# The last projection of a hybrid conformer and attention block: two full halves against seven products of quarters

## The chip, the core and the metric

The kernel runs on one core of a Trainium2 chip. The metric is the time of one execution on the device, in microseconds (us). Before the change it was 2436.01 us, the median of three runs (2435.82 to 2436.03).

## The reference, cut to what matters

The layer takes x of 2048 tokens by 1024 channels, runs a convolution branch and an attention branch, merges them into y (2048 x 1024), multiplies y by the output matrix, scales each output channel by a gate that is computed from the conditioning vector c, and adds x. Only the last lines are touched here:

```python
    mod = jax.nn.silu(c) @ w_ada + b_ada
    shift, scale, gate = jnp.split(mod, 3, axis=-1)
    ...
    y = jax.nn.sigmoid(m_conv) * y_conv + jax.nn.sigmoid(m_attn) * y_attn
    out = y @ w_out                                   # (2048 x 1024) by (1024 x 1024)
    x = (x + gate[:, None] * out).astype(dt)
```

## The kernel before, in words

Every large product is done in three terms. An operand is split into a high part, which ScalarE (ACT) rounds to the type that TensorE (PE) reads (a copy into `...h`), and a low part, which VectorE (DVE) or GpSimd (POOL) makes as the difference (`...l`). A product of two blocks is then high by high, high by low and low by high, all summed in one PSUM bank of 128 x 512.

The kernel works in stages. First come twelve attention units and the gates (`pz`, `pzg`, line 369). Then come the large input products (`quad`, line 944, its matmuls on line 954). These already use seven products of quarters in place of eight: three banks `pa`, `pb`, `pc` take the seven products in the order pa, pb, pa, pc, pa, pc, pa, and `PRODUCTS` (line 817) names which sum of data quarters meets which sum of weight quarters. After them come three stages with plain products through `project` (lines 1224 to 1230):

- `ya`: the attention output, four passes t = 0..3 of 512 tokens, eight blocks of 128 channels each;
- `yc`: the convolution output, again four passes of eight blocks of 24 matmuls. DVE gates each finished block (line 1390), adds the attention part `yl` (line 1391), and SyncE (SP) stores it to `y_d` in DRAM (line 1392);
- `out`: the last projection. It runs over 16 blocks `j` of 128 tokens. For each pair of blocks one load brings 256 tokens of y (`yw`, line 1400, 1 MB), ACT and DVE split a block (`yh`, `yl`, lines 1403 and 1404, 128 x 1024), and for each of the two column halves 24 matmuls (line 1230) fill a bank `out`. DVE multiplies it by the gate row (line 1413), adds x (line 1414), and SP stores the result (line 1415).

PE's order is the order of the program text up to the end of `yc` (`pe_order`, a manual schedule). A table `plan` with `at_block(n, m, f)` runs f ahead of matmul m of block n; the kernel uses it to place loads and splits that belong to a later stage. The instructions of the other engines are ordered by the scheduler that builds the program; each engine then runs its list strictly in order. In the last `yc` pass (t = 3) `split_wo` loads `w_out` in pieces of 128 x 512 (`fraw`, line 1107) and splits them into `wo0` and `wo1`, one for each column half.

Tiles come from pools; a tile that takes an older tile's place waits until the older one's last reader is done. Two such places matter below. `quarter_tile(kh, t, ...)` (line 226) hands out four-block areas of the old input; the second half of the convolution weights, `wc1`, lies in two of them and is read until the end of `yc`. The x tiles and the y blocks of the `yc` stage share four places (`yt`).

Of the kernel before, what the change touches and what calls it, by code (L numbers as in the profile page):

```python
# [10 lines left out]
F32 = mybir.dt.float32  # L11
F32R = mybir.dt.float32r
# [3 lines left out]
ALU = mybir.AluOpType  # L16
AX = mybir.AxisListType

P = 128
# [35 lines left out]
def tile_hybrid_block(  # L55
# [19 lines left out]
    def bank(tag, name):  # L75
        return psum.tile([P, 512], F32, tag=tag, name=name)
# [8 lines left out]
    ya_d = dram.tile([KC, P, S], F32, name="ya_d")  # L85
    y_d = dram.tile([KC, P, S], F32, name="y_d")
    gate_d = dram.tile([1, D], F32, name="gate_d")

    h_d = dram.tile([KC, P, S], F32, name="h_d")
    s_d = dram.tile([2, 4, 4, P, 512], F32, name="s_d")  # L90
# [1208 lines left out]
    def at_block(n, m, f):  # L1299
        plan.setdefault(n, {}).setdefault(m, []).append(f)  # L1300
# [11 lines left out]
    def load_wc(half, k, h, l):  # L1312
        split_big(h, l, w_conv_out[P * k : P * k + P, 512 * half : 512 * half + 512])
        wc[half][k] = h, l

    def load_wc0(k):
        if k < 4:
            return load_wc(0, k, *(wcp.tile([P, 512], F32R, name=f"wc0{hl}{k}") for hl in "hl"))
# [39 lines left out]
    last = {}  # L1358

    def split_wo(half, k):  # L1360
        h, l = (last["wo"][half].tile([P, 512], F32R, name=f"wo{half}{hl}{k}", bufs=1) for hl in "hl")
        split_big(h, l, w_out[P * k : P * k + P, 512 * half : 512 * half + 512])
        last[half, k] = h, l

    for t in range(NT):
        tsl = slice(512 * t, 512 * t + 512)
        if t == NT - 1:
            lnp_c.__exit__(None, None, None)
            wop_c, wop = right("wop")
            ap_c.__exit__(None, None, None)  # L1370
            up_c[1].__exit__(None, None, None)
            op_c = pool("op", bufs=2)
            op = op_c.__enter__()
            last["wo"] = wop, op
            gate_row = op.tile([P, D], F32, name="gate_row", bufs=1)
            nc.sync.dma_start(gate_row, gate_d.to_broadcast([P, D]))
            for k in range(KC):
                at_block(KC * t + k, 5, lambda k=k: split_wo(0, k))
                at_block(KC * t + k, 15, lambda k=k: split_wo(1, k))
        for dm in range(KC):  # L1380
            gt = gp.tile([P, 512], F32, tag="gt", name=f"mc{t}_{dm}")
            nc.sync.dma_start(gt, mc_d[dm, :, tsl])
            ya = ys.tile([P, 512], F32, tag="yt", name=f"yl{t}_{dm}", bufs=4)
            nc.sync.dma_start(ya, ya_d[dm, :, tsl])
            pz = bank("zso"[dm % 3], f"yc{t}_{dm}")
            sl = slice(P * (dm % 4), P * (dm % 4) + P)
            project(pz, [h[:, sl] for h, _ in wc[dm // 4]], [l[:, sl] for _, l in wc[dm // 4]],
                    norms[t].uh, norms[t].ul, plan.get(KC * t + dm))
            yt = ys.tile([P, 512], F32, tag="yt", name=f"yc{t}_{dm}", bufs=4)
            nc.vector.scalar_tensor_tensor(yt, gt, 1.0, pz, op0=ALU.add, op1=ALU.mult)  # L1390
            nc.vector.tensor_add(yt, yt, ya)
            nc.sync.dma_start(y_d[dm, :, tsl], yt)
    pe_order.__exit__(None, None, None)

    yw = None
    for j in range(NB):
        rows = slice(P * j, P * j + P)
        if j % 2 == 0:
            yw = sp.tile([P, S], F32, tag="wide", name=f"yw{j}").rearrange("p (k t) -> p k t", k=KC)
            nc.sync.dma_start(yw, y_d[:, :, P * j : P * j + 2 * P].rearrange("k p t -> p k t"))  # L1400
        src = yw[:, :, P * (j % 2) : P * (j % 2) + P]
        yh, yl = (op.tile([P, KC, P], F32R, tag=f"y{hl}", name=f"y{hl}{j}") for hl in "hl")
        nc.scalar.activation(yh, src, AF.Copy)
        nc.vector.tensor_sub(yl, src, yh.bitcast(F32))
        for half in range(2):
            cols = slice(512 * half, 512 * half + 512)
            xt = ys.tile([P, 512], F32, tag="fraw", name=f"xt{half}_{j}", bufs=3)
            nc.sync.dma_start(xt, x2[rows, cols])
# [3 lines left out]
            ot = op.tile([P, 512], F32, tag="ot", name=f"ot{half}_{j}", bufs=3)  # L1412
            nc.vector.tensor_tensor(ot, po, gate_row[:, cols], op=ALU.mult)  # L1413
            nc.vector.tensor_add(ot, ot, xt)
# [35 lines left out]
```

## Time and profile before

| what | value |
| --- | --- |
| time, median of 3 runs | 2436.01 us |
| the profiled execution: span from first to last instruction | 2433.6 us |
| median minus that span | 2.4 us |
| PE, share of the span busy | 98% |
| DVE, ACT, POOL busy | 69%, 40%, 32% |
| first matmul of the `out` stage, from the span's start | 2251.59 us |
| PE time of the `out` stage | 177.48 us, 768 matmuls |
| mean granted TensorE clock | 0.994 |

The profiled execution's own time is known as its span alone; the 2.4 us between the span and the median of the runs lie around it. Times in the profile count from the span's start. In a row of the trace, `out<-wo0h,yh` is an operation that writes tile `out` from `wo0h` and `yh`; what stands in square brackets is how long the engine had sat idle before it and what ended that. For a matmul the first name is the moving operand (the weights of the layer, 512 columns), the second is the stationary one (128 x 128 of y).

### The profile page before, as it was taken

How to read it: one execution, taken by the hardware profiler on the slowest of the kernel's cores; microseconds unless marked ns; L12 is line 12 of the kernel's file. 1: busy time of each engine (PE TensorE's matmuls, PEld its weight loads, DVE VectorE, ACT ScalarE, POOL GpSimd, SP SyncE). 2: the span in 40 equal slices, each digit the busy share in tenths (PEclk: the TensorE clock that was granted, in tenths of full speed). 3: DMA queues.
4: the chain of work that ended last, by engine and by line, in shares of the span. 5: the costliest groups of instructions: out<-in, count | busy, mean ns of one | idle time of the engine just before them, and what ended most of it. 6: DMA issues, size and time to landing. Idle time of an engine off the chain costs nothing.

```text
span 2433.6 us, 39444 instructions
## 1 busy us (share of the span) xinstructions
PE 2395.2 (98%) x12881; PEld 2138.5 (88%) x12881; DVE 1688.0 (69%) x3891; ACT 975.0 (40%) x2738; POOL 766.9 (32%) x899
## 2 busy tenths in 40 slices
PE   7999999999999999999999999999999999999999
PEld 3989999999999999999888888878888888888887
DVE  5855655555555565557779999989999968864333
ACT  5733333433344344345544444554444444331000
POOL 4421111111111111112467777765655620000000
PEclk8999999999999999999999999999999999999999
DMA  7633543444452222116663544664444479866443
GB/s 260 219 111 109 160 126 100 147 145 144 147 151 85 68 71 58 32 47 197 200 197 129 161 156 160 208 204 128 141 143 143 152 251 321 274 197 214 126 147 100
DMA packets 342219, 372.99 MB, mean 153 GB/s; under 512 B 29752, under 2 KB 243032, under 8 KB 342014
## 3 DMA queue, kind: packets, MB, share of 16 engines
q1 hardware_dynamic: 328718, 346.80, 45.9%
q10 hardware_dynamic: 13296, 23.66, 2.7%
q8 instruction: 103, 1.69, 0.3%
q14 instruction: 102, 0.84, 0.1%
HBM read 231.74 MB, written 138.61 MB: 152 GB/s over the span
## 4 chain that ended last, share of the span: by engine, by line
PE 92%; DVE 1%; ACT 1%; POOL 1%; DMA 1%; issue 0%; SPq 0%; POOLq 0%; DVEq 0%; ACTq 0%
PE pz L369 31%; PE yc L1230 7%; PE out L1230 7%; PE paab L954 7%; PE ya L1230 4%; PE pag_g_d L954 4%; PE pcab L954 4%; PE pag_mc_d L954 4%; PE pag_ma_d L954 3%; PE ps L441 3%; PE po L460 3%; PE pzg L369 3%; PE pbab L954 2%; PE pcg_mc_d L954 2%; PE pcg_g_d L954 2%; PE ptq L431 2%
## 5 line engine op out<-in xcount | busy, mean ns | idle before, releaser
L369 PE MATMUL pz<-wh_u,hT_lo 128*128 128x384 f32 x1536 | 537.6, 350 | 4.4 <-DVE hT_lo L288 2.5
L369 PE MATMUL pz<-wh_u,hT_hi 128*128 128x384 f32 x1536 | 519.5, 338 | 4.5 <-ACT wh_u L345 2.0
L369 PE MATMUL pz<-wl_u,hT_hi 128*128 128x384 f32 x1536 | 520.5, 339 | 0.4 <-DVE wl_u L348 0.4
L397 DVE SCALAR_TENSOR_TENSOR qk<-pz,st,wqk 128x128 f32<-128x128 f32 x384 | 117.0, 347 | 320.5 <-POOL st L113 320.4
L112 POOL TENSOR_SCALAR st<-st 128x2 f32<-128x2 f32 x192 | 47.7, 248 | 813.9 <-ACT sq L386 813.9
L369 PEld LDWEIGHTS pz<-wh_u,hT_hi 128*128 128x128 f32 x1536 | 291.5, 190 | 7.2 <-ACT wh_u L345 2.9
L369 PEld LDWEIGHTS pz<-wh_u,hT_lo 128*128 128x128 f32 x1536 | 290.0, 189 | 7.4 <-DVE hT_lo L288 3.2
L369 PEld LDWEIGHTS pz<-wl_u,hT_hi 128*128 128x128 f32 x1536 | 290.7, 189 | 1.9 <-DVE wl_u L348 1.4
L433 ACT ACTIVATE qkT<-ptq 128x256 f32<-128x256 f32 x192 | 73.9, 385 | 419.9 <-PE ptq L431 419.4
L1032 DVE SCALAR_TENSOR_TENSOR ce<-us,pair_taps,ce 128x512 f32<-128x512 f32 x240 | 180.3, 751 | 1.7
L1003 DVE SCALAR_TENSOR_TENSOR ce<-ut,chan,ce 128x512 f32<-128x512 f32 x240 | 180.1, 751 | 0.0
L1016 DVE SCALAR_TENSOR_TENSOR cq<-ut,chan,cq 128x512 f32<-128x512 f32 x208 | 156.6, 753 | 4.2
L918 POOL TENSOR_TENSOR slT<-wT,shT 128x512 fp32r<-128x512 f32 x97 | 128.7, 1328 | 75.7 <-ACT shT L917 74.6
L386 ACT ACTIVATE sq<-pz 128x128 bf16<-128x128 f32 x384 | 106.2, 276 | 100.3 <-PE pz L369 93.4
L113 POOL TENSOR_TENSOR st<-st,mhalf 128x2 f32<-128x2 f32 x192 | 136.5, 711 | 16.0
L917 ACT ACTIVATE shB<-wB 128x512 fp32r<-128x512 f32 x120 | 75.5, 630 | 150.4 <-issue 44.5
L917 ACT ACTIVATE shT<-wT 128x512 fp32r<-128x512 f32 x100 | 63.1, 631 | 153.1 <-issue 64.6
L918 POOL TENSOR_TENSOR slB<-wB,shB 128x512 fp32r<-128x512 f32 x77 | 102.0, 1324 | 68.0 <-ACT shB L917 66.4
L446 ACT ACTIVATE sm<-sm,osb 128x128 f32<-128x128 f32 (+1 forms) x192 | 88.8, 463 | 62.6 <-DVE osb L444 59.5
L1413 DVE TENSOR_TENSOR ot<-out,gate_row 128x512 f32<-128x512 f32 x32 | 22.1, 692 | 116.2 <-PE out L1230 116.2
L460 PE MATMUL po<-lv,pT 128*128 128x128 f32 x600 | 97.2, 273 | 0.0
L460 PEld LDWEIGHTS po<-lv,pT 128*128 128x128 f32 x600 | 93.0, 189 | 0.5 <-issue 0.5
(624 smaller groups left out, 6288.7 us busy)
## 6 DMA issues: line engine op xcount, KB each, us to landing
wB<-in_w_in_dram SPq DMA_DIRECT2D x140, 256.0 KB, 3.8
qkv_d<-qkv SPq DMA_DIRECT2D x128, 192.0 KB, 2.2
wT<-tT_d SPq DMA_DIRECT2D x80, 256.0 KB, 2.8
raw_u<-in_w_in_dram SPq DMA_DIRECT2D x93, 192.0 KB, 3.3
lqk<-qkv_d SPq DMA_DIRECT2D x128, 128.0 KB, 2.3
tT_d<-wB ACTq DMA_DIRECT2D x60, 256.0 KB, 2.3
acc_d<-osb SPq DMA_DIRECT2D x192, 65.0 KB, 1.6
at<-acc_d SPq DMA_DIRECT2D x64, 195.0 KB, 3.5
```

The source lines that it names most:

```text
L113: nc.gpsimd.tensor_tensor(dst, scratch[:, :n], mhalf[:, :n], op=ALU.pow)
L369: nc.tensor.matmul(pz[:, :width], part(a, k, P * j, P), w[:, :width], start=(m == 0), stop=(m == 23))
L386: nc.scalar.activation(sq, pz[:, P * i : P * i + P], AF.Square, scale=1.0 / math.sqrt(P), accum_out=st[:, i : i + 1])
L397: nc.vector.scalar_tensor_tensor(qk[:, 2 * i : 2 * i + 2].rearrange("p a b -> p (a b)"), pz[:, P * i : P * i + P], st[:, 2 + i : 3 + i], w ...
L460: nc.tensor.matmul(po[:, :P], box["pT"][:, P * i : P * i + P], vt, start=(i == 0), stop=(i == nk - 1))
L917: nc.scalar.activation(h, q[name], AF.Copy)
L918: eng.tensor_tensor(l, q[name], h.bitcast(F32), op=ALU.subtract)
L954: nc.tensor.matmul(ps, w, x, start=(m == 0 and ps.name not in first), stop=(m == 11 and not more), skip_group_check=True)
L1003: stt(box["e"], e[:, 1 + j : 513 + j], chan[:, cb, 2 * j : 2 * j + 1], box["e"], op0=ALU.mult, op1=ALU.add)
L1016: stt(box["o"], o[:, 2 + j : 514 + j], w, psum_o, op0=ALU.mult, op1=ALU.add)
L1032: stt(dst, box["both"][:, 1 + j : 513 + j], pair_taps[:, cb, j : j + 1], box["e"], op0=ALU.mult, op1=ALU.subtract if j == 0 else ALU.add)
L1230: nc.tensor.matmul(pz, w, xx, start=(m == 0), stop=(m == len(terms) - 1))
```

## The change

The last projection is done with the scheme of the large input products. y is cut in two by tokens (block j with block j + 8) and in two by channels; `w_out` is cut in two by rows and in two by columns. Each of eight steps j handles two token blocks and all 1024 columns with seven products of 12 matmuls. `PRODUCTS` is used as it stands, with `A` the quarters and sums of y and `B`, `T` the quarters and differences of `w_out`.

- PE's manual order now covers this stage too. The products run in the order 0, 3, 2, 1, 4, 5, 6 in the banks oa, oc, oa, ob, oa, oc, oa. A bank that is added to later is first read in between: DVE adds it into an x tile, which holds the output in the making. There are seven such adds of 128 x 512 in a step, and a store follows when an x tile is complete.
- `w_out` is multiplied by the gate when it is loaded (`wo_scale`, DVE, 128 x 1024 at a time), so the gate multiplication of the output is gone. POOL makes the differences `T1` to `T4` (`wo_first`), ACT and DVE split the seven matrices, which with their low parts take the places of older tiles. `B22` and `T4` take those of `wc1`, so their splits come in the first step (`out_hooks`).
- POOL makes the four sums of y in a step (`y_split`, four operations of 128 x 512), and ACT and DVE split seven sources of 128 x 512. `LEAD` = 5: the split for a product is emitted five products ahead.
- y is loaded as two loads of 128 tokens x 1024 channels per step (`yq`), x as four tiles of 128 x 512.

```diff
+    WO_ORDER = (0, 3, 2, 1, 4, 5, 6)
...
+    def wo_scale(k):
+        w = wo_raw[k]
+        for c in range(2):
+            nc.vector.tensor_tensor(w[:, :, c], w[:, :, c], last["gate"][c][:, None, :].to_broadcast([P, 2, 512]), op=ALU.mult)
...
+    def wo_first(k):
+        w = wo_raw[k]
+        wo_split("B11", k, w[:, 0, 0])
+        wo_split("B21", k, w[:, 1, 0])
+        t1 = ys.tile([P, 512], F32, tag="fraw", name=f"wot1_{k}", bufs=3)
+        for dst, x0, x1 in ((t1, w[:, 0, 1], w[:, 0, 0]), (w[:, 0, 0], w[:, 1, 1], w[:, 0, 1]), (w[:, 0, 1], w[:, 1, 1], t1),
+                            (w[:, 1, 0], w[:, 1, 0], w[:, 0, 1])):
+            nc.gpsimd.tensor_tensor(dst, x0, x1, op=ALU.subtract)
+        wo_split("T1", k, t1)
...
+    def y_split(j, i):
+        a11, a12, a21, a22 = (ysrc[j][:, q].rearrange("p k t -> p (k t)") for q in range(4))
+        pool_tt = nc.gpsimd.tensor_tensor
+        n = WO_ORDER[i]
+        if n == 0:
+            s1 = ysrc[j, "S1"] = ys.tile([P, 512], F32, tag="fraw", name=f"ys1_{j}", bufs=3)
+            pool_tt(s1, a21, a22, op=ALU.add)
+            pool_tt(a21, a11, a21, op=ALU.subtract)
+        if n == 2:
+            pool_tt(a11, ysrc[j, "S1"], a11, op=ALU.subtract)
+        if n == 4:
+            pool_tt(a12, a12, a11, op=ALU.subtract)
+        src = (a11, a12, a11, ysrc[j, "S1"], a21, a12, a22)[n]
...
+        nc.scalar.activation(h, src, AF.Copy)
+        nc.vector.tensor_tensor(l, src, h.bitcast(F32), op=ALU.subtract)
...
+        add = lambda dst, ps: nc.vector.tensor_tensor(dst, dst, ps, op=ALU.add)
...
+        product(0, pa, True)
+        add(x11, pa)
+        product(3, pc, True)
+        add(x22, pc)
+        product(2, pa, True)
+        add(x12, pa)
+        product(1, pb)
+        add(x11, pb)
+        store(0, x11)
+        product(4, pa, True)
+        add(x22, pa)
+        store(3, x22)
+        product(5, pc)
+        add(x12, pc)
+        store(1, x12)
+        product(6, pa)
+        add(x21, pa)
+        store(2, x21)
...
+    def out_hooks(j):
+        def f(i):
+            if j == 0 and i < 2:
+                for k in (2 * i, 2 * i + 1):
+                    wo_rest("B22", k, (nc.vector, nc.gpsimd)[k % 2])
+            elif j == 0 and i < 6:
+                wo_rest("T4", i - 2)
...
+            at = 7 * j + i + LEAD
+            if at < 7 * HB:
+                y_split(at // 7, at % 7)
...
-    yw = None
-    for j in range(NB):
...
-        nc.scalar.activation(yh, src, AF.Copy)
-        nc.vector.tensor_sub(yl, src, yh.bitcast(F32))
-        for half in range(2):
...
-            po = bank("zo"[half], f"out{half}_{j}")
-            project(po, [yh[:, k] for k in range(KC)], [yl[:, k] for k in range(KC)],
-                    [last[half, k][0] for k in range(KC)], [last[half, k][1] for k in range(KC)])
...
-            nc.vector.tensor_tensor(ot, po, gate_row[:, cols], op=ALU.mult)
-            nc.vector.tensor_add(ot, ot, xt)
-            nc.sync.dma_start(out2[rows, cols], ot)
```

The change moves instructions on all engines. On PE the two programs are the same up to the last matmul of `yc`; then 768 matmuls into `out` give way to 672 into `oa`, `ob` and `oc`. PE before, where the first column half of block 0 ends and the second begins:

```order
L1230 MATMUL out0_0_25460<-wo0l7_25417,yh0_25454 128x512
L1230 MATMUL out0_0_25460<-wo0h7_25416,yl0_25455 128x512
L1230 MATMUL out1_0_25491<-wo1h0_25117,yh0_25454 128x512
L1230 MATMUL out1_0_25491<-wo1l0_25118,yh0_25454 128x512
L1230 MATMUL out1_0_25491<-wo1h0_25117,yl0_25455 128x512
```

PE now, where the second product of step 0 (the sum S1 of y by T1, bank oc) ends and the third (S2 by T2, bank oa) begins; `yh0_3` is the high part of product 3's y operand in step 0:

```order
L1504 MATMUL oc0_25488<-wohT1_25125,yh0_3_25409 128x512
L1504 MATMUL oc0_25488<-wolT1_25126,yh0_3_25409 128x512
L1504 MATMUL oc0_25488<-wohT1_25125,yl0_3_25410 128x512
L1504 MATMUL oa0_25486<-wohiT2_25301,yh0_2_25473 128x512
L1504 MATMUL oa0_25486<-woloT2_25302,yh0_2_25473 128x512
L1504 MATMUL oa0_25486<-wohiT2_25301,yl0_2_25474 128x512
```

Before, a bank was filled once and read once. Now bank oa, which product 0 filled, is filled further here, and the matmul of the fourth row stands behind DVE's first read of it.

DVE before, from the last block of `yc` into the `out` stage:

```order
L1390 SCALAR_TENSOR_TENSOR yc3_7_25447<-mc3_7_25406,yc3_7_25410 128x512
L1391 TENSOR_TENSOR yc3_7_25447<-yc3_7_25447,yl3_7_25408 128x512
L1413 TENSOR_TENSOR ot0_0_25485<-out0_0_25460,gate_row_25089 128x512
L1414 TENSOR_TENSOR ot0_0_25485<-ot0_0_25485,xt0_0_25458 128x512
L1413 TENSOR_TENSOR ot1_0_25516<-out1_0_25491,gate_row_25089 128x512
```

DVE now, at the same place; `woloB22` and `woloT4` are low parts of the weights in the places of `wc1`, `yl0_5` is a low part of y, and the rows of L1491 are the adds into x:

```order
L1391 TENSOR_TENSOR woloB22_25502<-wo_raw0_24744,wohiB22_25501 128x512
L1391 TENSOR_TENSOR woloB22_25502<-wo_raw2_25107,wohiB22_25501 128x512
L1482 SCALAR_TENSOR_TENSOR yc3_7_25464<-mc3_7_25431,yc3_7_25435 128x512
L1432 TENSOR_TENSOR yl0_5_25511<-yq0_25309,yh0_5_25510 128x512
L1432 TENSOR_TENSOR yl0_6_25532<-yq0_25309,yh0_6_25531 128x512
L1483 TENSOR_TENSOR yc3_7_25464<-yc3_7_25464,yl3_7_25433 128x512
L1391 TENSOR_TENSOR woloT4_25549<-wo_raw0_24744,wohiT4_25548 128x512
L1391 TENSOR_TENSOR woloT4_25549<-wo_raw1_25105,wohiT4_25548 128x512
L1391 TENSOR_TENSOR woloT4_25549<-wo_raw2_25107,wohiT4_25548 128x512
L1491 TENSOR_TENSOR xt0_0_25349<-xt0_0_25349,oa0_25486 128x512
L1391 TENSOR_TENSOR woloT4_25549<-wo_raw3_25109,wohiT4_25548 128x512
L1491 TENSOR_TENSOR xt0_3_25351<-xt0_3_25351,oc0_25488 128x512
```

Splits of the weights and of y now stand ahead of the first add, for which PE's third product waits. The rows that follow on DVE lead up to the add ahead of product 6 of step 0, the last product of that step:

```order
L1432 TENSOR_TENSOR yl1_0_25556<-yq1_25507,yh1_0_25555 128x512
L1491 TENSOR_TENSOR xt0_1_25468<-xt0_1_25468,oa0_25486 128x512
L1432 TENSOR_TENSOR yl1_3_25583<-ys1_1_25552,yh1_3_25582 128x512
L1491 TENSOR_TENSOR xt0_0_25349<-xt0_0_25349,ob0_25487 128x512
L1432 TENSOR_TENSOR yl1_2_25604<-yq1_25507,yh1_2_25603 128x512
L1432 TENSOR_TENSOR yl1_1_25624<-yq1_25507,yh1_1_25623 128x512
L1432 TENSOR_TENSOR yl1_4_25643<-yq1_25507,yh1_4_25642 128x512
L1491 TENSOR_TENSOR xt0_3_25351<-xt0_3_25351,oa0_25486 128x512
```

Five splits of step 1's y, which need the load `yq1` and POOL's sums of it, stand among the adds of step 0. `yq1` takes the place of `wo_raw1`, so its load waits for the low part of T4 that reads `wo_raw1`. From step 1 on, each add alternates with one split.

More of the change, by code (lines that the diff above doesn't have):

```diff
@@ L1357, in tile_hybrid_block, with gate_rows @@
             at_block(KC * (t - 1) + k, 17, lambda t=t, k=k: norms[t].apply(k))
[L1358 to L1363, printed above, removed]
+    WO_ORDER = (0, 3, 2, 1, 4, 5, 6)
+    wo, wo_raw, last = {}, {}, {}
+    def gate_rows():
+        last["gate"] = [big["fr"].tile([P, 512], F32, tag="fraw", name=f"gate{c}", bufs=2) for c in range(2)]
+        for c in range(2):
+            nc.sync.dma_start(last["gate"][c], gate_d[:, 512 * c : 512 * c + 512].to_broadcast([P, 512]))
@@ new lines, in wo_split @@
+    def wo_split(name, k, src, eng=nc.vector):
+        if name not in wo:
+            wo[name] = wo_place(name)
+        h, l = (x[k] if isinstance(x, list) else x[:, k] for x in wo[name])
+        nc.scalar.activation(h, src, AF.Copy)
+        eng.tensor_tensor(l, src, h.bitcast(F32), op=ALU.subtract)
+    def wo_first(k):
[7 more added lines that the diff above has]
+        wo_split("T1", k, t1)
@@ new lines, in tile_hybrid_block, with out_quad, store, product @@
+    HB = NB // 2
+    def out_quad(j, hooks):
+        pa, pb, pc = bank("z", f"oa{j}"), bank("s", f"ob{j}"), bank("o", f"oc{j}")
+        x11, x12, x21, x22 = (xin.pop((j, q)) for q in range(4))
+        add = lambda dst, ps: nc.vector.tensor_tensor(dst, dst, ps, op=ALU.add)
+        begun = set()
+        def store(q, t):
+            jj, c = j + HB * (q // 2), q % 2
+            nc.sync.dma_start(out2[P * jj : P * jj + P, 512 * c : 512 * c + 512], t)
+        def product(n, ps, more=False):
+            yh, yl = ya_of.pop((j, n))
+            wh, wl = ([x[k] if isinstance(x, list) else x[:, k] for k in range(4)] for x in wo[PRODUCTS[n][1]])
+            yh, yl = ([y[:, P * k : P * k + P] for k in range(4)] for y in (yh, yl))
+            terms = [t for k in range(4) for t in ((yh[k], wh[k]), (yh[k], wl[k]), (yl[k], wh[k]))]
+            for m, (y, w) in enumerate(terms):
+                nc.tensor.matmul(ps, y, w, start=(m == 0 and ps.name not in begun), stop=(m == 11 and not more),
+                                 skip_group_check=True)
+            begun.add(ps.name)
+            hooks(WO_ORDER.index(n))
+        product(0, pa, True)
[16 more added lines that the diff above has]
+        store(2, x21)
```

83 lines of the change are left out of this document (66 added, 17 removed).

## The prediction

> **What bounds the kernel now.** I read the page's engine shares first, then the chain of work that ended last, then the windows of the last stages. Engine shares and chain by engine:
>
> ```profile
> span 2433.6 us, 39444 instructions
> ...
> PE 2395.2 (98%) x12881; PEld 2138.5 (88%) x12881; DVE 1688.0 (69%) x3891; ACT 975.0 (40%) x2738; POOL 766.9 (32%) x899
> ...
> PE 92%; DVE 1%; ACT 1%; POOL 1%; DMA 1%; issue 0%; SPq 0%; POOLq 0%; DVEq 0%; ACTq 0%
> ```
>
> PE is busy 98% of the span and is 92% of the chain. The change lies at the very end, so I take the chain there (start, length, what):
>
> ```profile
> 2199.82 51.77 PE yc L1230 x221
> 2251.59 177.48 PE out L1230 x768
> 2429.07 0.02 issue
> 2429.09 0.70 DVE ot L1413
> 2429.80 0.02 issue
> 2429.82 0.69 DVE ot L1414
> ```
>
> The `out` stage is one unbroken piece of 768 matmuls, 177.48 us, with no wait in it, and behind it stand two DVE operations and a store. Windows over the last `yc` pass and the `out` stage (length, busy time and instructions of each engine, granted clock, DMA share, GB/s), and over the first pass of `ya`:
>
> ```profile
> 2206.00:2251.00 45.00, 45.00 (x194) 36.18 (x193) 21.50 (x31) 8.80 (x13) 0.00 (x0) 1.00 0.73 237
> 2252.00:2429.00 177.00, 177.00 (x767) 143.50 (x765) 59.81 (x78) 14.84 (x14) 0.00 (x0) 1.00 0.41 127
> ```
>
> ```profile
> 1974.00:2018.00 44.00, 44.00 (x198) 35.60 (x196) 30.27 (x48) 17.10 (x29) 1.27 (x2) 1.00 0.99 339
> ```
>
> In both last windows PE is full at a granted clock of 1.00 while DVE, ACT and POOL have more than half their time free. So the stage costs what its matmuls cost: fewer of them save time as long as the other engines keep ahead.
>
> **The change part by part: the matmuls.** 8 steps of 7 products of 12 matmuls are 672 in place of 768, all 128 x 512. What one costs is not a single number in this trace. Pieces of the chain from the large input products, from `ya`'s first pass and from `yc`, then three matmuls of `out` that begin a column half:
>
> ```profile
> 1302.74 2.72 PE pbab L954 x12
> ...
> 1974.12 7.26 PE ya L1230 x32
> ...
> 2070.06 33.73 PE yc L1230 x144
> ```
>
> ```profile
> 2262.50 0.40 PE L1230 MATMUL out<-wo0h,yh 128*128 128x512 f32 x1
> ```
>
> ```profile
> 2268.11 0.40 PE L1230 MATMUL out<-wo1h,yh 128*128 128x512 f32 x1
> ```
>
> ```profile
> 2273.59 0.40 PE L1230 MATMUL out<-wo0h,yh 128*128 128x512 f32 x1
> ```
>
> From start to start that is 2.72/12 = 226.7 ns, 7.26/32 = 226.9 ns, 33.73/144 = 234.2 ns, and in `out` (2268.11 - 2262.50)/24 = 233.8 ns for the first half and (2273.59 - 2268.11)/24 = 228.3 ns for the second. The profile doesn't name the cause. One thing in the addresses of the built program runs with it: where the moving and the stationary operand have the same address modulo 64 bytes, the pitch is the short one (the input products, the first pass of `ya`, the second half of `out`), and where they differ by 32 it is the long one. In the built program of the change, only T1 (96 matmuls) agrees with its y tiles; the six others differ by 32. I therefore take 576 x 233.8 = 134.7 us and 96 x 228.3 = 21.9 us, together 156.6 us. The bounds are 672 x 226.7 = 152.3 us and 672 x 234.2 = 157.4 us.
>
> The Trainium skill ("TensorE: Matmul & The Clock Gate", Step-by-step: what each phase is for) gives a warm pitch of 512 columns divided by 2.4 GHz plus a fixed 2.5 ns, 215.7 ns. The trace disagrees, by 11 to 18 ns. By the page the stage would go from an estimated 165.7 us to an estimated 144.9 us, a saving of 20.8 us, nearly the same.
>
> **The work beside PE.** Prices of the other engines' operations (mean ns of one), and of DVE rows that follow each other:
>
> ```profile
> L1413 DVE TENSOR_TENSOR ot<-out,gate_row 128x512 f32<-128x512 f32 x32 | 22.1, 692 | 116.2 <-PE out L1230 116.2
> ...
> L1404 DVE TENSOR_TENSOR yl<-yw,yh 128x1024 fp32r<-128x1024 f32 x14 | 17.1, 1218 | 0.0
> ```
>
> ```profile
> L1403 ACT ACTIVATE yh<-yw 128x1024 fp32r<-128x1024 f32 x16 | 16.8, 1058 | 160.5 <-PE out L1230 160.5
> L1108 ACT ACTIVATE wo1h<-fraw 128x512 fp32r<-128x512 f32 x8 | 5.0, 631 | 27.4 <-PE yc L1230 18.3 <-DMA fraw<-in_w_out_dram 9.2
> ```
>
> ```profile
> L978 POOL TENSOR_TENSOR spare_hi<-spare_hi 128x512 f32<-128x512 f32 x5 | 6.5, 1299 | 0.0
> ```
>
> ```profile
> 2128.78 0.69 DVE L1289 SCALAR_TENSOR_TENSOR vf<-tv,gg 128x512 f32<-128x512 f32 x1
> 2129.39 0.69 DVE L1260 TENSOR_TENSOR red<-red,sq 128x512 f32<-128x512 f32 x1
> ```
>
> A DVE operation takes 0.69 us, and where the next one is ready it starts 0.61 us after it. A step of seven products lasts 156.6/8 = 19.6 us. In it DVE has 14 operations (9.7 us), ACT seven (4.4 us), POOL four (5.2 us): each fits in half a step. In the last `yc` pass, DVE gets 6 scalings of 128 x 1024 (7.3 us), 18 low parts of weights and 5 of y (15.9 us) beside its 16 `yc` operations (11.0 us): 34 us of 45. POOL gets 12 + 4 operations there, 21 us, and ACT 23, 14.5 us. All of it is due before the `out` stage begins, none of it is awaited by `yc`, and I cost it at nothing; the cover is the 45 us of matmuls. Removing that cover would put at most the excess of DVE's 34 us on PE. The scaling of the first piece (2.4 us of DVE) comes in the second `yc` pass, ahead of the last splits for the third:
>
> ```profile
> 2144.23 0.69 DVE L1292 TENSOR_TENSOR u_7l<-vf,u_7h 128x512 fp32r<-128x512 f32 x1
> ```
>
> The third pass begins two passes of 8 x 24 x 234.2 ns = 45.0 us before 2251.6, at 2161.7: the delayed split keeps over ten us.
>
> **The first step** is the tight place. I count from the end of `yc`, with a product at 2.80 us (T1: 2.74). ACT can split B22 from the middle of the last `yc` block, where its place comes free, and does so until -0.3; the two y sources after it end at 1.0, T4's four pieces at 1.6, 2.3, 2.9 and 3.5. DVE starts the last `yc` block at 0.0 and then, 0.61 apart, two low parts of y, the `yc` add and three pieces of T4. The first add into x starts at 4.3 and ends at 5.0. PE's third product needs it and could start at 5.54: slack 0.5 us. The load `yq1` waits for T4's second piece (3.7). Its landing I bound by a load of 256 KB of x, from issue to landing:
>
> ```profile
> DMA to landing us min/median/max: 2.6/2.7/3.3
> ```
>
> At the 339 GB/s of the window above, 256 KB more for a half of 512 KB takes 0.8 us: 3.5 us, the second half 1.6 later, so 7.3 and 8.9. The second add (behind one split) ends at 9.3, due at 11.1. For the third, POOL's sums end at 10.2, 11.5 and 12.8; three splits follow, the add ends at 16.1, and product 6 is due at 16.7. Slack 0.6 us. Below nothing PE's wait can't go, and above, each us by which `yq1` lands later is a us of PE, once. I take 0.5 us, since the slack is no more than the spread of landings; the high end is 5 us. From step 1 on, splits lead by five products, 14 us, and y loads are asked for a step or more ahead.
>
> **The end and the sum.** One add in place of two (0.71 us less); the store behind it is the same size. PE ends at 2251.6 + 156.6 + 0.5 = 2408.7, where it ended at 2429.07; the end after it was 2433.6 - 2429.1 = 4.5 us and becomes 3.8: span 2412.5. The median of the runs lies 2.4 above the span: 2414.9 us, 21.1 less than before.
>
> **The rivals.**
>
> *All matmuls at the short pitch.* Banks alternate from product to product, as in the input products, which run at 226.7. For it: those use the same three banks in nearly the same order. Against it: `ya`'s first pass fills one bank 12 matmuls long and is short, `out` alternates banks and is long half the time. 152.3 in place of 156.6: 2410.6 us.
>
> *The first step waits.* `yq1` lands 3 to 8 us later than summed, behind stores and x loads. DMA share is 0.73 in the window before, and the SP queue is in order. 2418 to 2424 us.
>
> *PE waits in every step: slower.* Ahead of product 6 of each step stands an add, ahead of it on DVE a split, ahead of that POOL, and POOL's list works up to three steps ahead, so that its sum for the step at hand can stand behind one whose load hasn't landed. The saving is 21.1/8 = 2.6 us a step; a wait longer than that in each step makes the change a loss. A wait of 3.5 us also lowers the clock. The input products show it (first a matmul behind a wait, its idle time in brackets; then the window after, clock 0.57; then that product's chain row):
>
> ```profile
> 1589.13 0.50 PE L954 MATMUL paab<-A_hi,shB 128*128 128x512 f32 x1 [3.51 <-ACT spare_hi L1080]
> ```
>
> ```profile
> 1590.00:1594.00 4.00, 4.00 (x12) 3.17 (x11) 3.93 (x6) 3.41 (x6) 2.61 (x2) 0.57 1.06 325
> ```
>
> ```profile
> 1589.13 4.42 PE paab L954 x12
> ```
>
> So one such wait costs 3.5 + (4.42 - 2.72) = 5.2 us; in eight steps 42 us: 2457 us. The Trainium skill ("TensorE: Matmul & The Clock Gate", Why this matters for your kernels) asks for no PE gap over about 3 us, else the clock falls; by that rule, the trace agrees. Against this rival: 14 us of lead and engines half idle.
>
> *That the change doesn't do what it says* is excluded for the count: the built order has 672 matmuls there.
>
> **How the numbers follow.** The forecast, 2412 to 2418, has a chance of 0.62; all short, 2410 to 2412, 0.12; waits in the first step or two, 2418 to 2424, 0.13; waits in every step 0.13, of which over half, 0.07, lies above 2440.9, 0.03 between 2431.1 and 2440.9, 0.03 below. A measurement of this kernel can tell about 0.2%, 4.9 us, from no change. So: faster 0.90, same 0.03, slower 0.07. The range is 2410 to 2421: the low end is the short pitch, the high end the forecast with some 6 us of waits.
>
> **What would show it.** Right: the first product starts at 2251.6 +- 0.5, PE's piece there is 156 to 158 us long for 672 matmuls, products by T1 are shorter than the others, PE's waits in the stage sum to under 1 us. Wrong: products of 2.72 us throughout; a wait of PE on the adds in step 0 of over 1 us; waits that return each step; a clock below 1.00 after 2251; a gap between `yc` and the first product.

## The result, and the profile after

The changed kernel takes 2426.14 us, the median of six runs (2423.47 to 2432.94), against 2436.02 us for the kernel before in the same comparison (six runs, 2435.82 to 2437.38). The ratio is 0.9962, with a 95% interval of 0.9951 to 0.9974: 9.9 us faster, where 21.1 us were forecast. The profiled execution is one of the quicker ones: 2423.63 us, span 2421.7 us, granted clock 0.994.

First the engine shares on the page of the changed kernel:

```profile
span 2421.7 us, 39474 instructions
...
PE 2372.0 (98%) x12785; PEld 2117.9 (87%) x12785; DVE 1734.9 (72%) x3941; ACT 998.0 (41%) x2790; POOL 839.7 (35%) x949
```

PE is busy 23.2 us less than before (2395.2), as 96 matmuls fewer should make it, but the span is only 11.9 us shorter (2433.6). So PE stands still somewhere. The list of PE's waits from the start of `ya` to the end (total, times, longest) has a single row:

```profile
PE oa L1504 <- DVE xt L1491: 8.9, 1, 8.9
```

One wait, 8.9 us long, for DVE's first add into an x tile. The first matmul of the stage in the timeline, and the chain (start, length, what), show the place:

```profile
2249.90 0.40 PE L1504 MATMUL oa<-wohB,yh 128*128 128x512 f32 x1
```

```profile
2261.99 1.81 DVE woloT L1391 x3
2263.79 0.61 DVE xt L1491
...
2264.53 5.21 PE oa L1504 x12
2269.74 2.81 PE ob L1504 x12
...
2283.75 2.76 PE oc L1504 x12
```

The `out` stage begins at 2249.90. Its third product, which could start 5.5 us later, starts at 2264.53, takes 5.21 us in place of 2.8, and from then on nothing waits: the products run at 2.80 us, those by T1 (the last row) at 2.76. Step 0 lasts 30.9 us, every later step 19.57 us. Windows over the last 45 us of `yc`, the wait, the product behind it, and the rest of the stage (length, busy time and instructions of PE, weight loads, DVE, ACT and POOL, granted clock, DMA share, GB/s):

```profile
2204.90:2249.90 45.00, 45.00 (x193) 36.17 (x192) 41.47 (x39) 15.11 (x26) 25.13 (x15) 1.00 0.59 195
2249.90:2264.40 14.50, 5.71 (x25) 4.32 (x23) 12.52 (x17) 3.23 (x6) 4.93 (x3) 0.82 0.56 174
2264.40:2270.00 5.60, 5.46 (x14) 4.36 (x15) 2.10 (x4) 1.26 (x2) 2.30 (x2) 0.56 1.12 334
2270.00:2417.80 147.80, 147.80 (x635) 118.85 (x634) 70.69 (x101) 29.50 (x47) 35.46 (x27) 1.00 0.45 142
```

DVE went from 21.50 us busy in its 45 us to 41.47, POOL from 0.00 to 25.13. But 39 DVE instructions at 0.69 us (1.22 for the six large ones) are 30 us, not 41. The groups of that window show which ones are dearer (count, busy time, mean ns of one, idle time before them):

```profile
L1375 DVE TENSOR_TENSOR wo_raw<-wo_raw,gate 128x1024 f32<-128x1024 f32 x6 | 9.8, 1666 | 0.9 <-DMA wo_raw<-in_w_out_dram 0.9
L1391 DVE TENSOR_TENSOR wolT<-wo_raw,wohT 128x512 fp32r<-128x512 f32 x4 | 6.9, 1774 | 0.0
...
L1482 DVE SCALAR_TENSOR_TENSOR yc<-mc,yc 128x512 f32<-128x512 f32 x7 | 4.8, 680 | 4.7 <-PE yc L1231 4.6
```

```profile
L1400 POOL TENSOR_TENSOR wo_raw<-wo_raw 128x512 f32<-128x512 f32 x6 | 10.5, 1760 | 2.1 <-DVE wolB L1391 2.0
```

An operation whose one operand is in PSUM (line 1482) costs what it did, 680 ns. One with both operands in SBUF costs 1774 ns, and POOL's cost 1760 instead of 1299. The timeline shows them side by side (start, length; DVE, then POOL):

```profile
2233.21 6.87 DVE L1391 TENSOR_TENSOR wolT<-wo_raw,wohT 128x512 fp32r<-128x512 f32 x4
2240.00 1.77 DVE L1483 TENSOR_TENSOR yc<-yc,yl 128x512 f32<-128x512 f32 x1
2241.70 0.68 DVE L1482 SCALAR_TENSOR_TENSOR yc<-mc,yc 128x512 f32<-128x512 f32 x1
2242.30 2.48 DVE L1391 TENSOR_TENSOR woloT<-wo_raw,wohiT 128x512 fp32r<-128x512 f32 x4
```

```profile
2234.39 3.44 POOL L1400 TENSOR_TENSOR wo_raw<-wo_raw 128x512 f32<-128x512 f32 x2
2237.79 1.74 POOL L1423 TENSOR_TENSOR yq<-yq 128x512 f32<-128x512 f32 x1
2239.61 1.62 POOL L1425 TENSOR_TENSOR yq<-ys,yq 128x512 f32<-128x512 f32 x1
```

While POOL runs its sums and differences, each engine takes 1.72 us an operation (DVE four in 6.87, POOL two in 3.44); POOL's last one ends at 2241.2, and the next four of DVE take 2.48 us together, 0.6 each. The thirteen operations of DVE in the last 45 us that have two SBUF operands and overlap none of POOL's take 0.67 to 0.69 us (1.21 to 1.23 for 128 x 1024). Summed over the rows from 2204.9 to 2263.7, DVE's operations with two SBUF operands take 16.8 us more than 0.69 and 1.22 us apiece. That is the main theory: **the two engines get in each other's way in SBUF**, DVE falls behind, and its first add is late. There are two rivals. *Late loads*: SP issues `yl` and the stores in order, and DVE also sat idle for loads and stores (2.8 and 0.9 us) just before the add. *Order on DVE*: the low parts of `B22` and T4 simply stand ahead of the first add.

### The profile page after: what moved, and what is told of

Same layout as the page of the kernel before. It is cut to its first block, busy times and chain, and to the rows that moved or that the text cites. A ratio compares the mean times of both kernels' runs of the same rounds, so it can differ in the third digit from the quotient of the medians.

```text
span 2421.7 us, 39474 instructions
## 1 busy us (share of the span) xinstructions
PE 2372.0 (98%) x12785; PEld 2117.9 (87%) x12785; DVE 1734.9 (72%) x3941; ACT 998.0 (41%) x2790; POOL 839.7 (35%) x949
## 5 line engine op out<-in xcount | busy, mean ns | idle before, releaser
L445 DVE CUSTOM_DVE_ANT_0 sm<-ps,mask 128x128 f32<-128x128 f32 (+1 forms) x192 | 68.7, 358 | 26.5 <-PE ps L442 26.4
```

## The experiments

PE's wait and the length of step 0 are those of each kernel's profiled execution; busy times are those of the last 45 us before the `out` stage. The stages ahead of it are not touched, and yet their length differs by several us from one profiled execution to the next: the first product starts at 2249.9 in the changed kernel, at 2254.9 and 2256.1 in two variants with the same products and addresses there. So wait and step 0 tell more than the total time.

| kernel | median us (runs) | ratio to before, 95% | PE's wait in the stage | step 0, us | later steps, us | DVE / POOL busy |
| --- | --- | --- | --- | --- | --- | --- |
| changed | 2426.14 (6) | 0.9962, 0.9951 to 0.9974 | 8.9 | 30.9 | 19.57 | 41.5 / 25.1 |
| no_diffs | 2417.53 (1) | one run | 1.6 | 21.6 | 19.57 | 34.3 / 9.3 |
| pool_one_input | 2415.69 (1) | one run | 1.2 | 21.0 | 19.57 | 39.6 / 27.3 |
| dve_diffs | 2419.07 (4) | 0.9929, 0.9913 to 0.9946 | 2.3 | 23.6 | 19.57 | 42.3 / 7.1 |
| pinned | 2423.01 (4) | 0.9948, 0.9933 to 0.9962 | 6.4 | 28.7 | 19.57 | 41.5 / 25.2 |
| pool_out | 2422.55 (4) | 0.9942, 0.9927 to 0.9956 | 3.9 | 24.2 | 19.57 | 39.9 / 0.0 |
| align | 2425.77 (4) | 0.9950, 0.9935 to 0.9965 | 8.7 | 30.4 | 19.27 | |
| pad64 | 2425.12 (1) | one run | 9.0 | 30.6 | 19.56 | |
| best2 | 2420.70 (4) | 0.9934, 0.9919 to 0.9949 | 5.8 | 27.0 | 19.27 | |
| dve_diffs_224 | 2419.39 (4) | 0.9924, 0.9907 to 0.9940 | 3.1 | 24.4 | 19.53 | |
| pool_out_96 | 2409.82 (4) | 0.9891, 0.9875 to 0.9908 | 5.1 | 25.0 | 19.04 | 39.8 / 0.0 |
| before_align | 2435.47 (10) | 0.9993, 0.9984 to 1.0003 | none | | | |
| before_96 | 2428.95 (6) | 0.9967, 0.9956 to 0.9979 | none | | | |

**no_diffs.** POOL's weight differences are gone.

```diff
-        t1 = ys.tile(...)
-        for dst, x0, x1 in (...):
-            nc.gpsimd.tensor_tensor(dst, x0, x1, op=ALU.subtract)
-        wo_split("T1", k, t1)
+        wo_split("T1", k, w[:, 0, 1])
```

> Leaves out the sixteen weight differences on POOL (T1, T2, T3, T4 are then split from gate-scaled weights, so the products are of other matrices); DVE keeps its list, its order and its loads. Contention theory (a DVE operation with two SBUF operands is stretched from 0.69 to 1.77 us while POOL runs one of its own): the DVE rows of the last yc pass are back at 0.69 us but for those beside the four y sums, DVE's busy time in its 45 us falls from 41.5 to at most 37 us, PE waits at most 1 us in step 0, no clock fall, span about 2411 us. Rival, late loads (SP's queue in order, yl lands late, 3.8 us of DVE idle on DMA): the loads are the same, so PE waits 3 to 9 us. Rival, order on DVE (the pieces of B22 and T4 stand ahead of the first add): list unchanged, so the wait stays over 5 us.

The window of the last 45 us, the same DVE group as above (its count holds T1's four splits too), and PE's waits:

```profile
2208.10:2253.10 45.00, 45.00 (x193) 36.17 (x192) 34.32 (x47) 15.54 (x28) 9.34 (x5) 1.00 0.71 238
```

```profile
L1391 DVE TENSOR_TENSOR wolT<-wo_raw,wohT 128x512 fp32r<-128x512 f32 x8 | 5.2, 686 | 0.0
```

```profile
PE oa L1500 <- DVE xt L1487: 1.6, 2, 1.2
```

DVE's list, order and loads are as they were, its rows are back at 686 ns, and it does 47 operations in less time than 39 before. The wait falls from 8.9 to 1.6 us; step 0 is 9.3 us shorter. Both rivals wanted a wait of 3 us or more: they fall as the main cause. The late loads were a consequence (their places came free late because DVE was late). Of the 1.6 us that are left, 1.2 stand at the first add and 0.3 ahead of product 6, where the chain goes through the load of `yq1` and POOL's sums of it. One more rival stays open here: without the differences, DVE's splits no longer wait for POOL's results either.

**pool_one_input.** POOL keeps its sixteen operations but reads one operand.

```diff
-            nc.gpsimd.tensor_tensor(dst, x0, x1, op=ALU.subtract)
+            nc.gpsimd.tensor_scalar(dst, x0, 1.0, None, op0=ALU.mult)
```

> The sixteen POOL differences become scalings by 1.0 of the first operand (the subtraction is left out, so the products are of other matrices): the same issues, places and nearly the same waits, but POOL reads one SBUF operand. Contention of any POOL operation on SBUF: DVE rows stay at about 1.77 us and PE's wait at 7 to 10 us. Contention only where POOL reads two operands: DVE rows 0.69 us, PE's wait at most 1 us, as without the differences. Late loads or order on DVE: the wait stays over 5 us with DVE rows at 0.69 us.

POOL's group in the last pass and step 0, a DVE operation beside one of its members, and PE's waits:

```profile
L1400 POOL TENSOR_SCALAR wo_raw<-wo_raw 128x512 f32<-128x512 f32 x9 | 15.1, 1702 | 0.2 <-DVE wolB L1391 0.2
```

```profile
2224.58 1.09 DVE L1483 TENSOR_TENSOR yc<-yc,yl 128x512 f32<-128x512 f32 x1
```

```profile
PE oa L1504 <- DVE xt L1491: 1.2, 1, 1.2
```

Neither reading holds. Beside such a scaling a DVE operation with two SBUF operands is stretched, but less: where it is hit, it takes 1.09 us in place of 1.77. In the last 45 us DVE loses 8.6 us, where it lost 14.2. Of the 8.6, only 3.7 stand beside the scalings (9.4 of the 14.2 stood beside the differences alone); the other 4.9 stand beside POOL's sums of y and low parts of `B22`, which still read two operands. POOL is hardly quicker (1702 ns). DVE does 47 operations in 39.6 us instead of 39 in 41.5, and the wait is as short as without the differences, although DVE's splits still wait for POOL's results here: that rival falls too. So the price depends on what POOL runs beside DVE, and isn't a yes or no. Whether it is the number of operands that counts, or something else in which the two operations differ, no run separates.

**dve_diffs.** DVE makes the differences.

```diff
-            nc.gpsimd.tensor_tensor(dst, x0, x1, op=ALU.subtract)
+            nc.vector.tensor_tensor(dst, x0, x1, op=ALU.subtract)
```

> The sixteen weight differences on DVE in place of POOL, nothing else. Contention theory: DVE gains sixteen operations 0.61 us apart (9.8 us) and loses about 13 of the 16.8 us by which its operations were stretched; its first add comes about 3 us earlier, PE waits 3 to 7 us in step 0 instead of 8.9, the time falls by 2 to 5 us to 2421 to 2424. DVE merely overloaded (prices unchanged by POOL): 9.8 us more work ahead of the first add, wait 15 to 19 us, time 2433 to 2437.

The window of the last 45 us, then PE's waits:

```profile
2209.90:2254.90 45.00, 45.00 (x194) 36.18 (x193) 42.25 (x58) 15.96 (x28) 7.13 (x5) 1.00 0.69 232
```

```profile
PE oa L1504 <- DVE xt L1491: 2.3, 1, 2.3
```

DVE is given sixteen operations more, does 58 in the window in place of 39, and is done sooner: 42.3 us busy against 41.5, and a wait of 2.3 us against 8.9. An overloaded DVE would have waited 15 us. The expectation (3 to 7 us) was itself too cautious, since DVE's idle time for late loads went too.

**pinned.** The first adds go ahead of the low parts of `B22` and T4.

```diff
+            i = nc.vector.tensor_tensor(dst, dst, ps, op=ALU.add)
+            if j == 0:
+                tc.keep_in_program_order(i)
...
+        if name in ("B22", "T4") and eng is nc.vector:
+            tc.keep_in_program_order(i)
...
-            if j == 0 and i < 2:
-                for k in (2 * i, 2 * i + 1):
+            if j == 0 and i in (1, 2):
+                for k in (0, 1) if i == 1 else (2, 3):
                     wo_rest("B22", k, (nc.vector, nc.gpsimd)[k % 2])
-            elif j == 0 and i < 6:
-                wo_rest("T4", i - 2)
+            elif j == 0 and i in (3, 4):
+                for k in (2 * i - 6, 2 * i - 5):
+                    wo_rest("T4", k)
```

> The first adds into x are kept on DVE ahead of the low parts of B22 and T4, which are issued one to two products later; POOL's differences stay. Order theory (only what stands ahead of the add matters): PE's wait falls from 8.9 to at most 0.5 us, time 2413 to 2416. Contention theory: the two pieces of B22 and three of T4 no longer stand ahead (5.2 us as stretched), the rest of the lateness stays: wait 3 to 5.5 us, clock fall if over 3 us, time 2418 to 2421.

PE's waits, then two low parts of y just ahead of the first add in DVE's timeline:

```profile
PE oa L1509 <- DVE xt L1494: 6.4, 2, 5.7
```

```profile
2259.88 2.76 DVE L1434 TENSOR_TENSOR yl<-yq,yh 128x512 fp32r<-128x512 f32 x2 [1.23 <-ACT yh L1433]
```

Order alone takes 2.5 of the 8.9 us: the add no longer stands behind those low parts, but DVE comes to it late all the same, and the two operations just ahead are again stretched beside POOL (2.76 us for two). The order theory (at most 0.5 us) falls. But 6.4 us is also more than the 3 to 5.5 that were expected under contention: 5.7 of them stand at the first add, and 0.7 came back at a later one.

**pool_out.** POOL has nothing to do in the last pass and step 0.

```diff
-            nc.gpsimd.tensor_tensor(dst, x0, x1, op=ALU.subtract)
+            nc.vector.tensor_tensor(dst, x0, x1, op=ALU.subtract)
...
-        pool_tt = nc.gpsimd.tensor_tensor
+        pool_tt = (nc.vector if j == 0 else nc.gpsimd).tensor_tensor
...
-                    wo_rest("B22", k, (nc.vector, nc.gpsimd)[k % 2])
+                    wo_rest("B22", k, nc.vector)
```

> The changed kernel with POOL out of the last yc pass and step 0: the weight differences, the y sums of step 0 and all four low parts of B22 on DVE; nothing is pinned and nothing padded. Contention theory: no DVE row over 0.75 us there (1.25 for 128 x 1024) though DVE has 24 operations more; the first add follows in time, PE waits 0 to 1 us in step 0, no clock fall; median 2412 to 2417, near the 2414.9 of the prediction. If DVE is overloaded in itself: wait over 5 us, 2420 or more.

The window, the DVE group again, and the first and the last of PE's three waits in the timeline (in brackets):

```profile
2211.10:2256.10 45.00, 45.00 (x193) 36.18 (x193) 39.88 (x61) 15.22 (x26) 0.00 (x0) 1.00 0.67 226
```

```profile
L1391 DVE TENSOR_TENSOR wolT<-wo_raw,wohT 128x512 fp32r<-128x512 f32 x4 | 2.7, 680 | 0.0
```

```profile
2263.14 0.48 PE L1504 MATMUL oa<-wohiT,yh 128*128 128x512 f32 x1 [1.29 <-DVE xt L1491]
...
2277.47 0.47 PE L1504 MATMUL oa<-wohiT,yh 128*128 128x512 f32 x1 [2.00 <-DVE xt L1491]
```

The mechanism is as expected: 61 operations of DVE in 39.9 us, those of 128 x 512 at some 680 ns. The time isn't: three waits sum to 3.9 us. What ended them is now something else. DVE sat idle 3.2 us behind a low part of y whose high part waits for a place that PE's last matmuls still read, and the fifth add stood behind y splits of step 1, whose load and sums were late. DVE's row, then pieces of the chain:

```profile
2252.08 0.69 DVE L1432 TENSOR_TENSOR yl<-yq,yh 128x512 fp32r<-128x512 f32 x1 [3.22 <-ACT yh L1431]
```

```profile
2259.84 4.10 DMA y_d<-yc
...
2264.39 5.89 DMA yq<-y_d
```

That is the prediction's rival of the late `yq1`, at a size of 2.0 us.

**align, pad64, before_align: the pitch.** The prediction read the pitch of a matmul from the addresses of its operands modulo 64. An unused tile of 32 bytes among the constants makes them agree everywhere; one of 64 bytes (`[P, 16]`) leaves them as they were.

```diff
+    pad = consts.tile([P, 8], F32, name="pad")
+    nc.gpsimd.memset(pad, 0.0)
```

> The changed kernel with one unused tile of 32 bytes a partition among the constants: it shifts the tiles behind it, so that moving and stationary operand agree modulo 64 bytes in all 672 matmuls of the output stage, all of ya and all of yc (576, 288 and 768 of them differed by 32). Address theory: products of 2.72 us in place of 2.80 (576 x 7 ns = 4.0 us less in the output stage), ya and yc 1056 x 7.3 ns = 7.7 us less, together about 12 us; step 0 keeps its wait of 8 to 11 us; median near 2414. Rival, the pitch comes from the order of banks or of operands: nothing changes, 2424 to 2428.

> Control: the same unused tile with 64 bytes a partition, which shifts the same tiles but leaves every address modulo 64 as it was. Address theory: products stay at 2.80 us (2.76 for T1), the time stays at 2423 to 2433. If shifting as such (or the added memset) does it: as the run with 32 bytes.

> The kernel before with the unused tile of 32 bytes. Address theory: ya and yc 7.7 us less, the 384 matmuls of the first column half 233.8 to 227 ns, 2.6 us less, the 384 of the second 0.5 us less: 10.8 us in all, median near 2425; no wait in the output stage. Rival, order of banks: unchanged, 2436.

The chain of the kernel before with the 32 bytes, then that of the changed kernel with them, then with the 64:

```profile
2071.29 33.60 PE yc L1232 x144
```

```profile
2289.67 2.75 PE ob L1506 x12
```

```profile
2071.20 33.59 PE yc L1233 x144
```

The theory half fell. `yc` went from 234.2 to 33.60/144 = 233.3 ns instead of 227, and the products from 2.80 to 2.75 us instead of 2.72. The 64 bytes did nothing to the steps (19.56 us), but brought `yc` to 33.59/144 = 233.3 ns just as the 32 did, so that part of the change can't be put down to agreement modulo 64. The times gained are within the spread of the runs. Modulo 256 the addresses say more: the operands of the input products and of `ya`'s first pass, the shortest of all, are equal modulo 256, while with 32 bytes `yc` still differs by 192 and the `out` products by 64.

**best2.** The edits of pool_out, pinned and align together; of them:

```diff
+    pad = consts.tile([P, 8], F32, name="pad")
...
+            nc.vector.tensor_tensor(dst, x0, x1, op=ALU.subtract)
...
+            if j == 0:
+                tc.keep_in_program_order(i)
```

> The changed kernel with POOL out of the last yc pass and step 0 (weight differences, y sums and pieces of B22 all on DVE), the first adds kept ahead of the low parts of B22 and T4, and the 32 byte tile. Contention theory: no DVE row over 0.75 us (1.25 for 128 x 1024), DVE's work of 46 us just fits its pass, PE waits 0 to 2 us in step 0; with the aligned addresses 12 us less and the wait of 8.9 us with its clock loss of 2.4 us gone: 2402 to 2406. Late loads or an overloaded DVE: the wait stays over 5 us, 2410 or more.

DVE's timeline ahead of the third add:

```profile
2266.97 0.69 DVE L1436 TENSOR_TENSOR yl<-yq,yh 128x512 fp32r<-128x512 f32 x1 [7.09 <-ACT yh L1435]
```

The first add is in time here (its row starts at 2255.59, 3.3 us after the first product). But the third add stands behind that y split, the first of step 1, for which DVE sat idle 7.1 us: PE waits 5.0 us there. From the chain:

```profile
2258.81 7.47 DMA yq<-y_d
```

The load of `yq1` was asked for behind seven loads of x, and its first half landed 7.47 us later. T4's low parts had no part in it: they came only after the third add, and in this program `yq1` takes the place of `yq0`. With the first wait gone, the next one showed.

**pool_out_96, before_96.** The unused tile has 96 bytes: equal modulo 256 in every matmul of 512 columns from the input products on.

```diff
+    pad = consts.tile([P, 24], F32, name="pad")
+    nc.gpsimd.memset(pad, 0.0)
```

> The same with an unused tile of 96 bytes among the constants, which makes the addresses of moving and stationary operand equal modulo 256 in every 512 column matmul from the input products on (with 32 bytes they agreed modulo 64, but differed by 192 modulo 256 in yc and by 64 in the output stage). Refined address theory (equal modulo 256, or 128, gives the short pitch): ya and yc 1056 x 7 ns = 7.5 us less, the output stage 576 x 4.5 ns = 2.6 us less: 10 us under the run without the tile, near 2404. Rival, addresses don't set the pitch: within 2 us of the run without the tile.

> The kernel before with the unused tile of 96 bytes. Refined address theory: the same 7.5 us in ya and yc and 384 x 4.5 ns = 1.7 us in the first column half: 9 us less, near 2427. Rival: within 2 us of the kernel before, as with 32 bytes.

From the chain of the first, then of the second:

```profile
2068.66 32.65 PE yc L1233 x144
...
2277.81 2.72 PE ob L1506 x12
```

```profile
2073.81 32.65 PE yc L1232 x144
```

32.65/144 = 226.7 ns in both, and products of 2.72 us throughout (a step 19.04 us). The changed kernel with POOL out of the way gains 12.7 us by 96 unused bytes (2422.55 to 2409.82), where 10 were expected, the kernel before 7.4 us (2436.34, nine runs, to 2428.95), where 9 were. So the rival, within 2 us, falls. pool_out_96 is the fastest of all, 26.5 us under the kernel before.

**dve_diffs_224.** Is it modulo 128 or 256? To dve_diffs comes:

```diff
+    pad = consts.tile([P, 56], F32, name="pad")
+    nc.gpsimd.memset(pad, 0.0)
```

> The weight differences on DVE (nothing else of POOL's moved, nothing pinned) and an unused tile of 224 bytes: moving and stationary operand then agree modulo 128 in every 512 column matmul, but differ by 128 modulo 256 in yc, in three quarters of ya and in all products of the output stage but those by T1. If agreement modulo 128 is what counts: products of 2.72 us throughout, yc at 226.7 ns, the time 10 us under the 2419 of the run without the tile, near 2409. If it must be modulo 256: products of 2.76 to 2.80 us except T1's, yc at 233 to 234 ns, 2417 to 2420. Contention theory for the rest: PE's wait in step 0 stays at 2 to 3 us, as in the run without the tile.

```profile
2072.20 33.46 PE yc L1233 x144
...
2279.50 2.73 PE oc L1506 x12
2285.03 2.80 PE ob L1506 x12
```

Modulo 128 is not enough: `yc` takes 33.46/144 = 232.4 ns, and only T1's products (first of the last two rows), whose operands agree modulo 256, are shorter. Wherever the addresses agree modulo 256 in these programs, they agree modulo 512 as well, so the runs don't tell these two apart. PE's wait of 3.1 us is near that of dve_diffs, as it should be.

## Why the prediction was wrong

It said 2414.9 us, range 2410 to 2421; the kernel took 2426.14. Point by point, on the span (2412.5 forecast, 2421.7 measured):

- *Matmuls and pitch: right.* 156.6/8 = 19.6 us a step were forecast and 19.57 measured, and T1's products are the shorter ones. The reading behind it was incomplete: equal modulo 64 is not enough; the short pitch came where they were equal modulo 256.
- *"The work beside PE ... I cost it at nothing": this step failed.* Its DVE sum, 34 us of 45, took the durations of an undisturbed DVE, and counted POOL's 21 us beside it as free. The two lists run at the same time on SBUF operands, and that stretched DVE's part by 16.8 us up to the first add. The sign stood in the old trace, in a group on DVE with two SBUF operands of 128 x 1024 whose mean is 1748 ns, not 1218. Thirteen of its fourteen operations run beside one of POOL's; the one that doesn't took 1214 ns:

```profile
L1043 DVE TENSOR_TENSOR usum<-usum,ca 128x1024 f32<-128x1024 f32 x14 | 24.5, 1748 | 0.3
```

  The window that I quoted for the last pass has POOL at 0.00, so prices from there could not be known to hold once POOL worked beside it.
- *The first step, slack 0.5 us.* The add was forecast to be done 5.0 us after the end of `yc`; it was done 14.5 us after (2264.4 - 2249.9). In place of 0.5 us PE waited 8.9, which is 8.4 more. No_diffs, dve_diffs and pool_out, which take POOL's work away in three ways, bring the wait to 1.6, 2.3 and 3.9: POOL's work beside DVE is worth 5 to 7.3 of the 8.9 us. Order on DVE is worth 2.5 us (pinned); the two overlap, since what stands ahead is itself stretched. The 1.6 us of no_diffs still have POOL's y sums and two low parts of `B22` beside DVE; how late a wholly undisturbed list in the same order would be was not run.
- *`yq1`.* The count, and the text ahead of the prediction, have its load wait for T4's second low part. In the changed kernel, as it is built, `yq1` takes the place of `yq0`, not of `wo_raw1` (that is so in pool_out and pool_out_96 alone). Its load was asked for when the last low part that reads `yq0` had ended (2261.39), while T4's second was still to come (2262.51):

```profile
2261.45 1.00 SPq L1413 DMA_DIRECT2D yq<-y_d  x2
```

  And the landing was counted too short: 3.5 us for the first half and 1.6 more for the second, where the second took 5.7 from its issue here, and a half 5.5 in no_diffs, 5.9 in pool_out and 7.5 in best2. In the changed kernel neither mattered, because the wait for the first add was longer.
- *The clock.* The product behind the wait took 5.21 in place of 2.81 us: 2.4 us, counted in the prediction only for a rival. Some 0.2 of them come behind any wait: behind 1.2 us, at a clock of 1.00, pool_one_input's product took 3.05. 8.4 + 2.4 = 10.8 us.
- *The start.* The first matmul of the stage came 1.5 us earlier than in the old trace (2249.90 against 2251.43 in the timeline; the chain's 2251.59 counts from the end of the matmul before it). A wait among the input products was 2.78 us long instead of 3.51, and the clock did not fall behind it. 10.8 - 1.5 = 9.3 us, against 9.2 us missing on the span. That the stage came earlier was luck, and hid as much of the error.
- *The end: right*, one add behind the last matmul.
- The other 2 us of the miss lie between the profiled execution (2423.63) and the median (2426.14). The six runs of the changed kernel differ by 9.5 us among each other, those before by 1.6; the two longest have a granted clock of 0.991, the two shortest 0.994. Only one of the six was profiled, so what the longer ones did stays open.

The rival "the first step waits" (2418 to 2424 us) had the place, and nearly the size; its cause, a late `yq1`, was not what ended the wait in the changed kernel, and showed only where POOL had less to do: 0.3 us in no_diffs, 2.0 in pool_out, 5.0 in best2. "PE waits in every step" did not happen: DVE's y splits are stretched there as well, but it has the time.

```profile
L1432 DVE TENSOR_TENSOR yl<-yq,yh 128x512 fp32r<-128x512 f32 x41 | 32.3, 791 | 1.3 <-ACT yh L1431 1.3
L1491 DVE TENSOR_TENSOR xt<-xt,oa 128x512 f32<-128x512 f32 x30 | 20.6, 688 | 44.6 <-PE oa L1504 44.6
```

These are groups of the stage from 2270 on: 791 ns for the splits, but 44.6 us of idle time ahead of the adds.

The Trainium skill ("SBUF — State Buffer", SBUF: two separate sides) says that a DVE operation with two SBUF inputs and a GpSimd operation that reads SBUF share a pair of ports under a lock, so that the one which comes second waits for the whole of the other. The traces agree as to who is hit (680 ns with a PSUM operand, 1774 with two in SBUF) and nearly as to the price: alternating, each took 1.72 us an operation, where 0.61 us for one of DVE and 1.36 for one of POOL (from start to start, each undisturbed) would make 1.97 one behind the other. They do not show that any reading of SBUF costs the same: beside a POOL operation with one operand, DVE's took 1.09 us in place of 1.77.

## What to carry to other kernels

Before work on DVE and POOL is called hidden because each has time, look whether the two would run at once on SBUF operands; if so, price DVE's at 1.7 us here in place of 0.6, or give POOL's to DVE, which took sixteen operations more and was done sooner. Where a chain of matmuls runs at a pitch longer than another of the same shape in the same kernel, compare the start addresses of moving and stationary operand modulo 256; 96 unused bytes were worth 7 to 13 us. And a slack of half a microsecond on an in-order queue is no slack: with one wait taken away (best2), another behind it in the same list came up.

## What the runs showed that was not expected

- The pitch of a 128 x 128 by 512 matmul depends on the addresses: in `yc` 226.7 ns when moving and stationary operand start equally modulo 256 bytes, and 232.4, 233.3, 233.3 and 234.2 ns when they differ by 128, 192, 224 and 160. In the `out` stage equal addresses gave 2.72 us a product, a difference of 64 gave 2.75 and of 32, 96 or 128 2.80; T1's equal products between others gave 2.73 to 2.76. Why is not known.
- What a wait costs through the clock isn't decided by its length alone. Among the waits of the input products and of the last stage in all these runs, none up to 2.10 us (best2) slowed the matmuls behind it, and each from 2.83 us (align) on did: from start to start they took 0.43 us in place of 0.23, for a while. In between both are found: behind 2.31 us (dve_diffs) the product took 1.7 us more, behind 2.78 us (the changed kernel, among the input products) none came more than 0.33 us after the one before. First dve_diffs in the chain, then the window behind the 2.78 us, with a clock of 1.00:

```profile
2262.90 4.53 PE oa L1504 x12
```

```profile
1588.30:1591.20 2.90, 2.88 (x12) 2.17 (x12) 2.86 (x5) 1.57 (x3) 1.82 (x2) 1.00 1.01 286
```

- POOL's operation with a single operand took 1702 ns beside DVE, hardly less than one with two (1760), while DVE's were stretched less. What it takes by itself no run shows.
